# Norm 2's residual set by ScalarE in the projection's banks, tile 0's right half turned over DRAM, and the first gate/up products in another order

## The chip, the cores and the metric

One core of one Trainium2 chip runs one decoder layer for 256 tokens. The time is device microseconds of an execution, the median of several runs. TensorE is PE in the rows, VectorE DVE, ScalarE ACT, GpSimd POOL, and SP is SyncE, which issues the DMAs here. The page gives the clock that PE was granted in each slice of the span; in the kernel before it is the full one throughout.

## The reference, cut to what matters

`h` is (256, 1024) in float32, and so are all weights. The part that the change touches is the end of the cross-attention, the second norm and the beginning of the feed-forward layer:

```python
s = einsum('bshd,bmhd->bhsm', q, k) * (256 ** -0.5)      # 4 heads of 256, 256 memory tokens
p = softmax(s, axis=-1)
o = einsum('bhsm,bmhd->bshd', p, v).reshape(B, S, D)
h2 = layer_norm(DEEPNORM_ALPHA * h1 + o @ w_xo, ln2_g, ln2_b)
out = layer_norm(DEEPNORM_ALPHA * h2 + (silu(h2 @ w_gate) * (h2 @ w_up)) @ w_down, ln3_g, ln3_b)
```

`h1` is the output of the first norm, `D_FF` is 2816.

## The kernel before

**Tokens and products.** The 256 tokens are two tiles t of 128. A float32 product is made of three products of halves (L399 to L401): a matrix is split into a rounded high half (a ScalarE cast) and the rest, a low half (a VectorE subtraction), and high by high, low by high and high by low are summed in PSUM. `split` does this for activations (L527 on ScalarE, L528 on VectorE).

**Weights.** All weights come as one stream of numbered tiles w0, w1, ... of 128x1024 elements, 0.524 MB each. `Stream` loads a raw tile by a DMA on SyncE's queue (L125) into one of 7 raw buffers, splits it (`prepare`: ScalarE's cast L149, VectorE's subtraction L151) into one of 9 pairs of high and low tiles, and `refill` issues the load of the next raw tile into the buffer that the split frees. So w80's load waits for w73's low half, and w70's cast waits until TensorE has used w61 for the last time. `ws.late` keeps `refill` from running until it is called. Parameters of the norms (`ln2_g`, `ln2_b`, L369) are loaded on the same queue just ahead of given weights.

**The stages.** The four heads' queries are projected (`do_xq`), the scores of a head (`xscores`) go through a softmax, and its probabilities are transposed over DRAM: `xprobs_out` transposes blocks of 32 x 32 on VectorE (L560) and writes them, `xprobs_in` gathers them (xr) by four DMAs, `xprobs_split` makes the two halves xst, and `xattend` multiplies them with the values into the bank xo, which is split into oT. The output projection `project(c_xo, ...)` takes w51 to w58 into four banks acc, one for each piece: token tile 0 or 1, left or right half of the 1024 columns. With w51 to w54 it works on all four pieces at once, with w55 to w58 it finishes one piece after another. Then Norm 2 (`Norm`): for each piece the sum `alpha * h1 + acc` goes to r (L901), `bn_stats` measures it (L908, with a small addition at L910), `stats` joins both halves (L915) and GpSimd makes the reciprocal root (L917), `centre` (L922) and `scale` (L928) write h2.

**Gate and up.** h2 is needed transposed, as h2Th and h2Tl: eight TensorE transposes for tile 0 (L548), four for the left half of tile 1 (L538), while the right half of tile 1 is turned over DRAM (h2s, h2d, h2r). Gate and up are computed in chunks c of 256 columns each, chunk 0 with w59 to w62, chunk 1 with w63 to w66, chunk 2 with w67 to w70. `gated` makes silu(gate) times up (sg, L1188 and L1189), `gated_out` and `gated_in` turn it over DRAM (gs on VectorE, the write gd, four gathers gr at L571), `token_sums` makes sums of its blocks on GpSimd (L1208 to L1213), their split S goes into `shared_products`, with products of sums of the rows of w_down (w71, w72 for chunk 0) into four shared banks x.

**The order.** Each engine works through its instructions in the order in which this code issues them; there is no reordering. The generators (`project`, `proj_n`, `by_row`) issue some products at each step, so `run(gen, n)` followed by something else sets what stands behind what. `until(xo)` runs the projection until the next piece is finished. In the first chunks `run(gu, ...)` in the loop over c runs `by_row`, which goes through what is left of chunk 1, and `gated_in(0)` stands behind its third step.

## Time and profile before

| what | value |
|---|---|
| runs | 361.06, 361.18, 361.82 us; median 361.18 |
| profiled execution | 361.86 us, its span 360.1 |
| PE busy | 354.3 us (98%), 1768 instructions |
| DVE busy | 320.2 us (89%), 494 instructions |
| ACT busy | 208.6 us (58%), 335 instructions |
| POOL busy | 69.0 us (19%), 77 instructions |
| DMA | 90.80 MB, mean 252 GB/s |

The span is what the trace covers; 1.76 us of the execution lie around it. Times within the trace count from the start of the span. A matmul's start is measured and its end is modelled, so gaps on PE are read from one start to the next. An entry such as "[0.61 <-DVE xst L528]" behind an instruction says that its engine sat idle for 0.61 us before it, and that DVE's writing of xst at line 528 ended the wait.

### The profile page before, as it was taken

What the parts mean: (1) busy time and instruction counts of PE and PEld (TensorE: products, weight loads), DVE (VectorE), ACT (ScalarE), POOL (GpSimd) and SP (SyncE); (2) the same over time, 40 slices, a digit from 0 to 9 for tenths busy, and PEclk for the clock granted to TensorE, in tenths of its full rate; (3) what the DMA queues carried; (4) which work ended last, traced back from release to release, by engine and by line L of the source; (5) the groups of instructions that cost most, each with busy time, mean ns of one, the idle gap of its engine ahead of it and who ended that gap; (6) DMA issues with size and microseconds to landing.
All of it is one profiled execution on the core that took longest, in us unless ns stands there. A gap on an engine that the chain in (4) does not pass through costs nothing. (4 is left out here: it accounts for less than half of the span.)

```text
span 360.1 us, 5338 instructions
## 1 busy us (share of the span) xinstructions
PE 354.3 (98%) x1768; PEld 299.3 (83%) x1768; DVE 320.2 (89%) x494; ACT 208.6 (58%) x335; POOL 69.0 (19%) x77
## 2 busy tenths in 40 slices
PE   9999999999999999999999999999999999999995
PEld 8887888888888888988888888888888888888883
DVE  4888999987999877778999969999999999879995
ACT  5867775576363646557227627646744754675922
POOL 1000009400000000000010025044224304403284
PEclk9999999999999999999999999999999999999999
DMA  7997378799935955429918787697889889677113
GB/s 232 417 419 307 116 283 334 218 341 314 374 144 191 396 211 204 165 77 303 365 39 313 251 302 251 222 321 271 299 288 305 292 272 338 211 225 243 52 66 117
DMA packets 38748, 90.80 MB, mean 252 GB/s; under 512 B 4416, under 2 KB 16832, under 8 KB 38592
## 3 DMA queue, kind: packets, MB, share of 16 engines
q1 hardware_dynamic: 38288, 90.20, 70.7%
q8 instruction: 14, 0.23, 0.2%
q10 hardware_dynamic: 432, 0.26, 0.2%
q14 instruction: 14, 0.11, 0.1%
HBM read 82.58 MB, written 7.86 MB: 251 GB/s over the span
## 5 line engine op out<-in xcount | busy, mean ns | idle before, releaser
L1208 POOL TENSOR_TENSOR sraw<-gr 128x128 f32<-128x128 f32 x10 | 9.8, 976 | 103.2 <-DMA gr<-gd 63.6
L917 POOL TENSOR_TENSOR rs<-mv,mhalf 128x1 f32<-128x1 f32 x6 | 3.8, 634 | 115.0 <-DVE mv L915 115.0
L764 POOL TENSOR_TENSOR win<-upad 128x271 f32<-128x271 f32 x4 | 3.5, 882 | 52.3 <-DVE upad L801 52.3
L1188 ACT ACTIVATE sg<-pg 128x256 f32<-128x256 f32 x22 | 7.6, 379 | 5.9 <-PE pg L401 5.9
L1210 POOL TENSOR_TENSOR sraw<-gr 128x128 f32<-128x128 f32 x10 | 10.9, 1094 | 0.0
L528 DVE TENSOR_TENSOR gTl<-gr,gTh 128x512 fp32r<-128x512 f32 x11 | 8.9, 805 | 1.9 <-ACT gTh L527 1.9
L527 ACT CAST S<-sraw 128x384 fp32r<-128x384 f32 (+1 forms) x10 | 5.3, 533 | 8.5 <-POOL sraw L1210 8.5
L527 ACT CAST gTh<-gr 128x512 fp32r<-128x512 f32 x11 | 6.8, 615 | 4.5 <-DMA gr<-gd 4.5
L1209 POOL TENSOR_TENSOR sraw<-sraw,gr 128x128 f32<-128x128 f32 x10 | 9.2, 918 | 0.8
L1189 DVE TENSOR_TENSOR sg<-sg,pg 128x256 f32<-128x256 f32 x22 | 8.3, 412 | 0.1
L668 ACT ACTIVATE pr<-pr,mx 128x256 f32<-128x256 f32 (+1 forms) x12 | 5.5, 460 | 4.5 <-DVE mx L714 4.5
L560 DVE STREAM_TRANSPOSE gs<-sg 128x512 f32<-128x512 f32 x11 | 7.7, 702 | 0.1
L1213 POOL TENSOR_TENSOR S<-gr,sraw 128x128 f32<-128x128 f32 x8 | 7.5, 940 | 0.0
L922 DVE SCALAR_TENSOR_TENSOR r<-r,mv,g 128x512 f32<-128x512 f32 (+1 forms) x10 | 7.0, 729 | 0.2
L527 ACT CAST h2Th<-tp 128x512 fp32r<-128x512 f32 x3 | 1.7, 588 | 9.4 <-PE tp L548 6.7
L528 DVE TENSOR_TENSOR S<-sraw,S 128x384 fp32r<-128x384 f32 (+1 forms) x10 | 6.1, 606 | 1.0 <-ACT S L527 0.9
L165 POOL TENSOR_TENSOR w138l<-t,w138h 128x1024 fp32r<-128x1024 f32 x1 | 4.2, 4211 | 13.1 <-ACT w138h L164 13.1
L908 DVE BATCH_NORM_STATS2 st<-r 128x6 f32<-128x512 f32 (+1 forms) x10 | 6.4, 636 | 0.3
L1057 PE MATMUL xs<-xkTh,xq 128*128 128x256 f32 x32 | 6.4, 283 | 0.0
L527 ACT CAST h1T<-hr 128x512 fp32r<-128x512 f32 x4 | 2.3, 619 | 6.8 <-DMA hr<-hd 6.8
L527 ACT CAST xst<-xr 128x512 fp32r<-128x512 f32 x4 | 2.5, 619 | 6.3 <-DMA xd<-xs 3.6
L528 DVE TENSOR_TENSOR xst<-xr,xst 128x512 fp32r<-128x512 f32 x4 | 2.8, 688 | 3.8 <-ACT xst L527 3.8
(1390 smaller groups left out, 1378.9 us busy)
## 6 DMA issues: line engine op xcount, KB each, us to landing
gd<-gs SPq DMA_DIRECT2D x11, 256.0 KB, 5.8
gr<-gd SPq DMA_DIRECT2D x44, 64.0 KB, 2.0
pd<-ps SPq DMA_DIRECT2D x4, 384.0 KB, 4.1
pt<-pd SPq DMA_DIRECT2D x16, 96.0 KB, 5.7
g<-in_ln_g SPq DMA_DIRECT2D x3, 512.0 KB, 8.1
b<-in_ln_b SPq DMA_DIRECT2D x3, 512.0 KB, 9.6
wr<-in_w_qkv SPq DMA_DIRECT2D x5, 256.0 KB, 5.0
mr<-in_mem_t SPq DMA_DIRECT2D x1, 1024.0 KB, 11.8
```

The source lines that it names most:

```text
L527: nc.scalar.copy(h, ps)
L528: nc.vector.tensor_sub(l, ps, r32(h))
L560: nc.vector.transpose(st[:, :, at:at + m, :].rearrange("p j m b -> p m j b"), src.rearrange("p m (j b) -> p m j b", b=32))
L908: nc.vector.bn_stats(self.st[:, self.n, :], x)
L922: nc.vector.scalar_tensor_tensor(r, r, self.mv[:, 0:1], gb["g", self.i][:, s], op0=OP.subtract, op1=OP.mult)
L1057: nc.tensor.matmul(ps[:, t, :], w, xkT[n][:, 2 * h + kk], start=not (low or t or kk or n), stop=bool(low and kk), skip_group_check=True)
L1188: nc.scalar.activation(sg, ps[:, :CW].rearrange("p (f b) -> p f b", f=2), AF.Silu, bias=0.0, scale=1.0)
L1189: nc.vector.tensor_mul(sg, sg, ps[:, CW:].rearrange("p (f b) -> p f b", f=2))
L1208: nc.gpsimd.tensor_add(s1, a21, a22)
L1209: nc.gpsimd.tensor_sub(s2, s1, a11)
L1210: nc.gpsimd.tensor_sub(s3, a11, a21)
L1213: nc.gpsimd.tensor_sub(s4_raw, a12, s2)
```

## The change

Four things are changed together.

*The residual.* `residuals()` lets ScalarE write alpha times h1 into the four banks of the output projection before its first product, between the splits of the probabilities of heads 0 and 1; the projection then accumulates on top. The four sums L901 of Norm 2 are gone, and `bn_stats` and `centre` read the banks themselves. So that the banks are free, head 3's queries go to other ones, and the bank of head 2's scores is allocated ahead.

*Head 3.* `xprobs_split(3)` is issued ahead of the split of w60 instead of behind it.

*Tile 0's turn.* The right half of tile 0's h2 goes over DRAM as tile 1's does (`h2_out`, `landed`, `h2_split`), and four transposes instead of eight remain. The parameters of Norm 2 are loaded two and three weights earlier, and the load of w69 and w70 is issued behind the turn of tile 0.

*Order of gate and up.* Tile 0 of chunks 0 and 1 is interleaved in another way, the transposes of tile 1 move a few rows, and what is left of chunk 1's tile 0 (w65 and w66) is issued ahead of w61 and w62 of chunk 0's tile 1. `by_row` then has only tile 1 of chunk 1 left.

```diff
-    ws.before(c_gu[1][3], load_norm("g", 2, ln2_g))
-    ws.before(c_gu[2][0], load_norm("b", 2, ln2_b))
+    ws.before(c_gu[1][1], load_norm("g", 2, ln2_g))
+    ws.before(c_gu[1][2], load_norm("b", 2, ln2_b))
...
-        def centre(self, c0, c1, r=None):
+        def centre(self, c0, c1, r=None, src=None):
             s = slice(c0, c1)
             r = self.r[:, s] if r is None else r
-            nc.vector.scalar_tensor_tensor(r, r, self.mv[:, 0:1], gb["g", self.i][:, s],
+            nc.vector.scalar_tensor_tensor(r, r if src is None else src, self.mv[:, 0:1], gb["g", self.i][:, s],
...
-    def project(chunks, get, held, pieces=PIECES):
-        acc = {piece: accbank("acc") for piece in PIECES}
+    def project(chunks, get, held, pieces=PIECES, acc=None):
+        fresh = acc is None
+        if fresh:
+            acc = {piece: accbank("acc") for piece in PIECES}
...
-            yield from proj_rows(acc, head, get, PIECES, True, pieces != PIECES, True)
-        ws.prepare(ws.used + AHEAD)
+            yield from proj_rows(acc, head, get, PIECES, fresh, pieces != PIECES, True, not fresh)
+        if fresh:
+            ws.prepare(ws.used + AHEAD)
...
+    def residuals():
+        for piece in PIECES:
+            t, c0, c1 = piece
+            xo_acc[piece] = accbank("acc")
+            nc.scalar.mul(xo_acc[piece], h1[:, t, c0:c1], ALPHA)
...
+    ahead[2] = bank("xs")
     run(xq[3], 4)
     xprobs_split(0)
+    residuals()
     run(xq[3], 2)
     rest = xscores(2)
     xprobs_split(1)
...
     run(xo, 1)
+    xprobs_split(3)
     prepare()
     run(xo, 2)
-    xprobs_split(3)
-    prepare()
     xattend(2)
     xattend(3)
     prepare()
+    ws.late = True
+    prepare()
...
+    def h2_out(t):
+        return turned([(0, h2[:, t, 512:].rearrange("p (k b) -> p k b", k=4))], 4, "h2")
+    def h2_split(t, raw):
+        h, l = [half[:, 4:, t * P:(t + 1) * P].rearrange("p k (i b) -> p k i b", i=4) for half in h2T]
+        split(h, l, raw.rearrange("p i k b -> p k i b"))
...
-    for half in HALVES:
-        norm.add(*half, until(xo)[1])
-    norm.finish()
+    acc00 = until(xo)[1]
+    norm.take(acc00)
+    prepare()
+    acc01 = until(xo)[1]
+    norm.take(acc01)
+    norm.stats()
+    norm.centre(*RIGHT, src=acc01)
+    norm.centre(*LEFT, src=acc00)
+    norm.scale(*RIGHT)
+    turn0 = h2_out(0)
+    norm.scale(*LEFT)
...
+    turn0 = landed(turn0, 4, "h2")
+    ws.fetch(len(ws.raws) + 2, nc.sync)
     run(xo, 3)
-    norm.add(*HALVES[0], acc0)
-    transposes_tok(h2T, h2[:, 0, :], 0)
-    acc1 = until(xo)[1]
-    norm.add(*HALVES[1], acc1)
+    prepare()
+    transpose_tok(h2T, h2[:, 0, :], 0, 0, lambda: None)
+    acc11 = until(xo)[1]
+    run(xo)
+    norm.take(acc10)
+    norm.take(acc11)
     norm.stats()
...
+    norm.centre(*RIGHT, src=acc11)
+    norm.centre(*LEFT, src=acc10)
+    h2_split(0, turn0)
+    norm.scale(*RIGHT)
+    turn1 = h2_out(1)
+    norm.scale(*LEFT)
+    turn1 = landed(turn1, 4, "h2")
+    prepare()
+    ws.refill()
...
-    run(proj_n({0: first[0]}, c_gu[0], h2T, False, 2))
+    gu0 = proj_n({0: first[0]}, c_gu[0], h2T, False, 2)
+    run(gu0, 4)
     run(gu1[0], 4)
-    transpose_tok(h2T, h2[:, 1, :], 1, 0, lambda: (ws.prepare(ws.next()), gated(0, 0, first[0])))
-    run(gu1[0], 2)
-    gu0 = proj_n({1: first[1]}, c_gu[0], h2T)
+    run(gu0, 3)
+    transpose_tok(h2T, h2[:, 1, :], 1, 0, lambda: None)
+    run(gu0)
+    gated(0, 0, first[0])
+    gu0 = proj_n({1: first[1]}, c_gu[0], h2T, True, 2)
     run(gu0, 4)
-    ws.prepare(ws.next())
-    h, l = [half[:, 4:, P:].rearrange("p k (i b) -> p k i b", i=4) for half in h2T]
-    split(h, l, turn2.rearrange("p i k b -> p k i b"))
+    prepare()
+    run(gu1[0])
+    h2_split(1, turn1)
     ws.held = False
     run(gu0)
```

VectorE from the split of w60 to Norm 2 of tile 0; rows with + stand in the kernel after alone, with - in the one before alone; xst are head 3's probabilities, oT the heads' outputs:

```order
+L528 TENSOR_TENSOR xst<-xr,xst 128x512
 L151 TENSOR_TENSOR w60l<-w60r,w60h 128x1024
-L528 TENSOR_TENSOR xst<-xr,xst 128x512
+L528 TENSOR_TENSOR oTl<-xo,oTh 128x512 x2
 L151 TENSOR_TENSOR w61l<-w61r,w61h 128x1024
-L528 TENSOR_TENSOR oTl<-xo,oTh 128x512 x2
 L151 TENSOR_TENSOR w62l<-w62r,w62h 128x1024
+L908 BN_STATS st<-acc 128x6
+L910 TENSOR_SCALAR st<-st 128x1
 L151 TENSOR_TENSOR w63l<-w63r,w63h 128x1024
```

Head 3's low half moves ahead of w60's, both outputs' low halves ahead of w61's, and the first statistics ahead of w63's.

TensorE in chunk 0's tile 1, where w66 of chunk 1's tile 0 now ends and w61 follows:

```order
+L399 MATMUL pg<-w66h,h2Th 128x512
+L400 MATMUL pg<-w66l,h2Th 128x512
+L401 MATMUL pg<-w66h,h2Tl 128x512
 L399 MATMUL pg<-w61h,h2Th 128x512
 L400 MATMUL pg<-w61l,h2Th 128x512
 L401 MATMUL pg<-w61h,h2Tl 128x512
```

The six products of w66 for tile 0 stood behind w62's of tile 1 before, and now stand ahead of w61's and w62's.

SyncE's queue around the gathers of chunk 0 (gr from gd):

```order
 L125 DMA w78r<-in_w_down 128x1024
 L125 DMA w79r<-in_w_gu 128x1024
+L125 DMA w80r<-in_w_gu 128x1024
 L571 DMA gr<-gd 32x4x128 x4
-L125 DMA w80r<-in_w_gu 128x1024
 L125 DMA w81r<-in_w_gu 128x1024
```

w80's load was issued behind the four gathers and is now issued ahead of them.

## Rows read from the trace of the kernel before

**Rows 1.** Part 1 of the page: busy us (share of the span), instructions of each engine.

```profile
PE 354.3 (98%) x1768; PEld 299.3 (83%) x1768; DVE 320.2 (89%) x494; ACT 208.6 (58%) x335; POOL 69.0 (19%) x77
```

**Rows 2.** Timeline of PE at head 3: start, duration, engine, line, operation, out<-in, shape [idle].

```profile
165.73 0.28 PE L399 MATMUL xo<-xst,xv 128*128 128x256 f32 x1
166.62 0.39 PE L400 MATMUL xo<-xst,xv 128*128 128x256 f32 x1 [0.61 <-DVE xst L528]
166.85 0.28 PE L401 MATMUL xo<-xst,xv 128*128 128x256 f32 x1
...
167.92 0.28 PE L401 MATMUL xo<-xst,xv 128*128 128x256 f32 x1
```

**Rows 3.** Timeline of PE at the transposes of Norm 2's output (tp).

```profile
178.27 1.03 PE L548 MATMUL tp<-ident,h 128*128 128x128 f32 x8
179.06 0.48 PE L399 MATMUL acc<-w58h,oTh 128*128 128x512 f32 x1
...
179.84 0.39 PE L488 MATMUL pg<-w59h,h2Th 128*128 128x512 f32 x1
...
188.00 0.60 PE L538 MATMUL tp<-ident,h 128*128 128x128 f32 x4
188.36 0.48 PE L399 MATMUL pg<-w65h,h2Th 128*128 128x512 f32 x1
```

**Rows 4.** Timeline of ACT: casts of probabilities, outputs, a weight and transposed halves.

```profile
148.09 0.62 ACT L527 CAST xst<-xr 128x512 fp32r<-128x512 f32 x1 [2.69 <-DMA xr<-xd]
...
168.24 0.59 ACT L527 CAST oTh<-xo 128x512 fp32r<-128x512 f32 x1 [1.73 <-PE xo L401]
168.72 1.06 ACT L149 CAST w62h<-w62r 128x1024 fp32r<-128x1024 f32 x1
...
188.64 0.59 ACT L527 CAST h2Th<-tp 128x512 fp32r<-128x512 f32 x1 [2.78 <-PE tp L538]
...
190.69 0.62 ACT L527 CAST h2Th<-h2r 128x512 fp32r<-128x512 f32 x1 [0.51 <-DMA h2r<-h2d]
```

**Rows 5.** Timeline of DVE in Norm 2 of tile 0, and tile 1's transpose.

```profile
170.96 1.22 DVE L151 TENSOR_TENSOR w63l<-w63r,w63h 128x1024 fp32r<-128x1024 f32 x1
172.09 0.68 DVE L901 SCALAR_TENSOR_TENSOR r<-h,acc 128x512 f32<-128x512 f32 x1
172.80 0.70 DVE L908 BATCH_NORM_STATS2 st<-r 128x6 f32<-128x512 f32 x1
...
175.15 0.21 DVE L915 BATCH_NORM_AGGREGATE mv<-st 128x2 f32<-128x12 f32 x1
175.40 1.44 DVE L922 SCALAR_TENSOR_TENSOR r<-r,mv,g 128x512 f32<-128x512 f32 x2
176.76 1.40 DVE L928 SCALAR_TENSOR_TENSOR h<-r,rs,b 128x512 f32<-128x512 f32 x2
...
184.58 0.71 DVE L560 STREAM_TRANSPOSE h2s<-h 128x512 f32<-128x512 f32 x1
```

**Rows 6.** Timelines of all five engines on the way to chunk 0's sums S.

```profile
194.13 1.06 ACT L149 CAST w70h<-w70r 128x1024 fp32r<-128x1024 f32 x1
195.71 1.21 DVE L151 TENSOR_TENSOR w70l<-w70r,w70h 128x1024 fp32r<-128x1024 f32 x1
...
203.13 1.21 DVE L151 TENSOR_TENSOR w73l<-w73r,w73h 128x1024 fp32r<-128x1024 f32 x1
...
204.81 1.80 SPq L571 DMA_DIRECT2D gr<-gd  x4
...
210.34 0.46 POOL L1208 TENSOR_TENSOR sraw<-gr 128x128 f32<-128x128 f32 x1 [26.71 <-DMA gr<-gd]
...
212.78 0.56 DVE L528 TENSOR_TENSOR S<-sraw,S 128x384 fp32r<-128x384 f32 x1 [0.90 <-ACT S L527]
...
214.10 0.39 PE L401 MATMUL x<-w71h,S 128*128 128x512 f32 x1
```

**Rows 7.** Windows: us, busy (count) of PE, PEld, DVE, ACT, POOL, PEclk, DMA share, GB/s.

```profile
203.00:212.00 9.00, 9.00 (x41) 7.48 (x40) 6.98 (x9) 3.73 (x6) 1.58 (x3) 1.00 0.85 275
```

More of the change, by code (lines that the diff above doesn't have):

```diff
@@ L956, in project @@
             yield from proj_rows(acc, rest, lambda k: get(done + k), [piece], not head or piece[1] % 512 != 0, True,
-                                 piece == pieces[-1], bool(head) and pieces != PIECES)
+                                 piece == pieces[-1], bool(head) and (pieces != PIECES or not fresh))
             yield piece, acc[last] if pieces != PIECES and piece == pieces[-2] else acc[piece]
@@ L1038, in do_xq @@
     def do_xq(h):
-        pss = [halved((accbank if h else bank)("pxq")) for f in range(2)]
+        pss = [halved((accbank if h in (1, 2) else bank)("pxq")) for f in range(2)]
         yield from proj_w(pss, c_xq[h], h1T)
@@ L1048, in do_xq @@
         split(*xqT[h], sums)
+    ahead, xo_acc = {}, {}
+    def residuals():
[3 more added lines that the diff above has]
+            nc.scalar.mul(xo_acc[piece], h1[:, t, c0:c1], ALPHA)
     def xscores(h):
-        ps = bank("xs").rearrange("p (t s) -> p t s", t=2)
+        ps = (ahead.pop(h, None) or bank("xs")).rearrange("p (t s) -> p t s", t=2)
         for low in range(2):
@@ L1130, in decoder_layer @@
     h2 = ap.tile([P, T, D], F32, tag="a8", name="h2")
-    xo = project(c_xo, lambda k: (oT[0][:, k], oT[1][:, k]), 4)
+    xo = project(c_xo, lambda k: (oT[0][:, k], oT[1][:, k]), 4, acc=xo_acc)
     xattend(0)
@@ L1156, in decoder_layer @@
     prepare()
+    ws.late = True
+    prepare()
     h2T = (a8("h2Th", F32R), a8("h2Tl", F32R))
     gT = [(a8(f"gTh{i}", F32R), a8(f"gTl{i}", F32R)) for i in range(3)]
[L1161 to L1164 removed]
+    LEFT, RIGHT = HALVES
+    def h2_out(t):
[3 more added lines that the diff above has]
+        split(h, l, raw.rearrange("p i k b -> p k i b"))
+    norm = Norm(2, h1[:, 0, :], h2[:, 0, :])
+    acc00 = until(xo)[1]
[9 more added lines that the diff above has]
+    norm.scale(*LEFT)
     norm = Norm(2, h1[:, 1, :], h2[:, 1, :])
[L1166 removed]
+    acc10 = until(xo)[1]
     warm = sp.tile([P, 32], F32, name="warm", bufs=1)[:, :1]
     nc.scalar.activation(warm, mhalf, AF.Silu, bias=0.0, scale=1.0)
+    turn0 = landed(turn0, 4, "h2")
+    ws.fetch(len(ws.raws) + 2, nc.sync)
     run(xo, 3)
[L1170 to L1182 removed]
+    prepare()
[4 more added lines that the diff above has]
+    norm.take(acc11)
+    norm.stats()
+    norm.centre(*RIGHT, src=acc11)
[7 more added lines that the diff above has]
+    ws.refill()
     def gated(c, t, ps):
@@ L1262, in decoder_layer @@
     sgs = [sp.tile([P, 2, T, P], F32, name="sg", tag="pr", bufs=PR_BUFS)]
-    first = [accbank("pg") for t in range(T)]
-    second = [accbank("pg") for t in range(T)]
+    first, second = zip(*[[accbank("pg") for n in range(2)] for t in range(T)])
     gu1 = [proj_n({t: second[t]}, c_gu[1], h2T, t == 1) for t in range(T)]
-    run(proj_n({0: first[0]}, c_gu[0], h2T, False, 2))
+    gu0 = proj_n({0: first[0]}, c_gu[0], h2T, False, 2)
+    run(gu0, 4)
     run(gu1[0], 4)
-    transpose_tok(h2T, h2[:, 1, :], 1, 0, lambda: (ws.prepare(ws.next()), gated(0, 0, first[0])))
-    run(gu1[0], 2)
-    gu0 = proj_n({1: first[1]}, c_gu[0], h2T)
+    run(gu0, 3)
[3 more added lines that the diff above has]
+    gu0 = proj_n({1: first[1]}, c_gu[0], h2T, True, 2)
     run(gu0, 4)
-    ws.prepare(ws.next())
-    h, l = [half[:, 4:, P:].rearrange("p k (i b) -> p k i b", i=4) for half in h2T]
-    split(h, l, turn2.rearrange("p i k b -> p k i b"))
+    prepare()
+    run(gu1[0])
+    h2_split(1, turn1)
     ws.held = False
```

8 lines of the change are left out of this document (removed).

## The prediction

> **What bounds the kernel now.** I read the page first: TensorE is busy for 354.3 us of a span of 360.1 [rows 1], so it sets the time, and anything else counts only where it makes TensorE wait or takes instructions from it. Then I went through TensorE's timeline for gaps between the starts of its products. In the stretch that the change touches they follow each other every 0.227 us (512 columns; some 40 in 9.00 us, where [rows 7] counts 41 with those cut at the ends) or 0.12 us (256 columns: half of that, and 0.01) with one exception: at head 3 of the cross-attention a product starts 0.89 us after the one before it, named as waiting for VectorE's low half of the probabilities, and the next comes 0.23 us later instead of 0.12 [rows 2]. The transposes of the Norm 2 output are the other thing there that is not a product [rows 3]. From there I followed each input of the stretch back through the timelines of ScalarE, VectorE, SyncE's queue and GpSimd, to see how much later it could come without TensorE noticing. The profiled execution took 361.86 us, its span 360.1, so 1.76 lie around it; it is 0.68 above the median of 361.18. I take differences within the execution and add them to the median. 0.2%, about what a measurement of this kernel can tell from no change, is 0.72 us.
>
> **What it takes off TensorE.** (1) Head 3's probabilities are split one weight tile earlier on ScalarE and VectorE. The low half before started only behind the low half of w60; now it ends about where that one started its last part, before TensorE comes to it. The exception goes: 0.89 − 0.12 and 0.23 − 0.12 make 0.77 + 0.11 = 0.88 us [rows 2]. (2) Four of eight transposes of tile 0 go to the DMA: eight took from 178.27 to 179.06, 0.79 us, four from 188.00 to 188.36, 0.36 us [rows 3]; so 0.43 us. Together −1.31.
>
> **What costs nothing.** The four scaled copies of h1 into the projection's banks are about 0.6 us each by the nearest row, a ScalarE cast of 512 (0.59 to 0.62 us), 2.4 in all; they stand behind the cast of head 0, ahead of which ScalarE idled 2.69 us waiting for its data [rows 4], and what follows them on ScalarE is a cast whose data also lands only later. If that cover were gone they would hold the products of head 0's neighbours by up to 2.4 us, but all of it would have to be exposed at once. The four sums on VectorE go (0.68 us each, [rows 5]); VectorE has no way to pass that on directly, it only starts its next step earlier. The gate/up products are the same in number, so their new order is worth something only through waits.
>
> **What it adds: transposes behind Norm 2.** (3) The last product of head 3 started at 167.92 [rows 2]; without the stall it starts at 167.04, and the transposes would come at 178.27 − 0.88 = 177.39. Norm 2 of tile 0 on the other engines then runs so: ScalarE's cast of head 3's output follows the product by 0.32 us as before (168.24 − 167.92), 167.36; w61's high half, which now stands behind it instead of ahead, 0.48 later (168.72 − 168.24), 167.84 [rows 4]; its low half when that cast of 1.06 is done, 168.93; two low halves of 1.13 each (170.96 to 172.09), 171.2; statistics 0.73 (0.70 and the 0.03 between instructions); the small addition 0.18 (what is left of 172.80 to 175.15 after two statistics of 0.73 and one sum of 0.71); w63's low half 1.13; statistics 0.73; aggregate 0.25 (175.15 to 175.40); two centres 1.36 (175.40 to 176.76); one scale 0.70; the new 32 x 32 transpose 0.63 to 0.71 (184.58's row); one scale 0.70 [rows 5]. The left half is there at 177.7 to 177.8. Wait 0.4, and after a wait the first product cost 0.11 extra [rows 2]: 0.5 us. Bounds: 0, if ScalarE or VectorE gets one step ahead of this, and 0.8, if a weight's cast slips by a third of its 1.06. A gain is excluded, as nothing is taken away here that (1) and (2) have not counted.
>
> [...]
>
> (4) Behind each of the two groups of four transposes TensorE has one row of three products of other data and then needs the ScalarE cast of what was transposed. The cast started 0.64 us behind the transposes (188.64 − 188.00) and takes 0.59 [rows 3, 4]; with 0.06 to the product, 1.29 us. TensorE gets there after 0.36 + 0.78 = 1.14 us (179.06 to 179.84 are the three products, [rows 3]). Wait 0.15, with the 0.11 of a restart 0.25, twice 0.5 us; bounds 0 and 0.8. So far TensorE: −0.88 − 0.43 + 0.5 + 0.5 = −0.3.
>
> The right half of tile 0 goes over SyncE's queue: five DMAs, ahead of two weight loads. By the row of the gathers of chunk 0 four issues take 1.80 us [rows 6], and for tile 1's right half, which went this way before, 6.1 us lay between the start of its transpose at 184.58 and the cast of what landed, which began at 190.69 [rows 4, 5]. From the new transpose at 176.3 that makes 182.4; it is needed behind 24 products of gate/up, which begin some 1.4 behind the transposes, at 177.8 + 1.4 + 24 × 0.227 = 184.6: no wait. Weights w69 and w70 move back behind the turn, to some 181, and w70 is cast only at 194.13 [rows 6].
>
> **What it adds: chunk 0's token sums come later.** (5) This is where I see the result decided. Today the low half of the sums S of chunk 0 is done at 212.78 + 0.56 = 213.34, and TensorE uses it at 214.10: 0.76 us to spare [rows 6]. That alone caps any gain ahead of it: with 0.06 to the product and 0.11 of a restart TensorE can't be there more than about 0.6 earlier unless S comes earlier too. And S comes later, for two reasons. First, six products of w66 (1.36 us) now stand ahead of w61's last use, which comes 1.36 − 0.3 = 1.06 later. w70's cast waits for that buffer; it started at 194.13, as that product ended, and will at 195.19; its low half follows after its 1.06, at 196.25 instead of 195.71: VectorE's row through w73's low half, done at 204.34, moves by +0.5 [rows 6]. Second, the order on SyncE's queue: w80's load, which waits for w73's low half to free its raw buffer, now stands ahead of chunk 0's four gathers, which were issued at 204.81 and landed when GpSimd began at 210.34. They can now be issued only at 204.34 + 0.5 + 0.45 (one issue, a quarter of 1.80) = 205.3, +0.5, and w80's 0.524 MB are ahead of them. Price of that: nothing, if the DMA engines carry both side by side (they were 85% busy here), up to 0.524 MB / 275 GB/s = 1.9 us, if the gathers wait for all of it at this stretch's rate [rows 7]. The gathers took 5.5 us from issue to landing though they are small, so they do stand behind other loads, yet they are spread over four issues; I take the middle, +1.0. Landing +1.5 (bounds 0.5 and 2.4), S low at 214.84. TensorE's own path brings it there at 214.10 − 0.3 = 213.8: wait 214.84 + 0.06 − 213.8 = 1.1, with the restart 1.2. Sum: −0.3 + 1.2 = **+0.9 us**, with the bounds −0.1 (landing +0.5: wait 0.2) and +1.8 (landing +2.4: wait 2.1). Since S decides, the terms (1) to (4) hardly enter the result: whatever TensorE saves ahead it waits for here. Later chunks have more to spare, and TensorE is back to back behind, so I carry +0.9 to the end.
>
> [...]
>
> **Rivals.** A: w80's load doesn't hold the gathers up and VectorE's row makes up part of the 0.5. Then S costs 0 to 0.2 and the change is worth its TensorE terms, −0.1 to −0.6, about 360.9. For it: the DMA engines have 15% to spare and SyncE only waits some 0.5 longer. Against: 5.5 us for small gathers. B, on the other side: the waits (3) and (4) don't arise and S doesn't bind, −1.3, 359.9. The point from which it decides: S must be ready by 214.10 − 1.31 = 212.79, 0.55 earlier than today, so the gathers must land by 209.7, although they are issued later; only an emptier queue at 203 us could do that. For it: the raw loads are kept back around Norm 2, so fewer may be in flight; against: 275 GB/s there [rows 7] and the same bytes before it. [...] D: the change doesn't do what it says, head 3's split still being late because its data, by its own turn over DRAM, lands too late for the earlier place. Then up to 0.88 stay and w61, w73 and S move with them: +0.9 + 0.88 = +1.8, 363.0. For it: the split moves up by a whole weight tile. Against: before, ScalarE's cast of it had no wait of its own that the trace names.
>
> **How the numbers follow.** Forecast (S decides, w80's load in the way) 0.53, A 0.25, B 0.13, C 0.05, D 0.04. The predicted time is 361.18 + 0.9 = 362.1; that case alone spans 361.1 to 363.0. The range, 360.5 to 363.0, takes in A and leaves out most of B and the far end of D. Slower by over 0.72 us: two thirds of the forecast (0.35), C and most of D, 0.43. Faster by over 0.72: B and a little of A, 0.15. The rest, 0.42, within.
>
> **What would show it.** Right: no gap at head 3's products; four transposes; waits of some tenths ahead of the first transposes and ahead of the first product on each transposed half; the gathers issued behind w80, landing near 211.8; a wait of about 1 us at the first product with S's low half. Wrong: S's low half there in time (A, B), the gathers landing where they landed before, or a wait in a place that I have not named, above all later, where VectorE has the least to spare.

## The result

The changed kernel is slower: a median of 363.32 us (8 executions, 362.62 to 365.23) beside 361.62 for the kernel before (8 executions, 361.06 to 362.99), a ratio of 1.0054 with a 95% interval of 1.003 to 1.0077, or 1.1 to 2.8 us. The forecast was 362.1 with a range of 360.5 to 363.0: slower was the likelier side, but the size was about half of it, and the range ends too low.

In the profiled execution of the changed kernel the span is 361.7 us, 1.6 more than before. TensorE's timeline (start, duration, engine, line, operation, out<-in, shape, and in brackets the idle time and what ended it) shows the waits that were added, one after the other; the transposes, its second row, answer to 178.27 in [rows 3]:

```profile
177.33 0.39 PE L401 MATMUL acc<-w57h,oTl 128*128 128x512 f32 x1
177.89 0.63 PE L538 MATMUL tp<-ident,h 128*128 128x128 f32 x4 [0.17 <-DVE h L928]
178.28 0.48 PE L399 MATMUL acc<-w58h,oTh 128*128 128x512 f32 x1
...
178.82 0.40 PE L401 MATMUL acc<-w58h,oTl 128*128 128x512 f32 x1
179.20 0.50 PE L488 MATMUL pg<-w59h,h2Th 128*128 128x512 f32 x1
179.53 0.40 PE L488 MATMUL pg<-w59l,h2Th 128*128 128x512 f32 x1
...
212.53 0.39 PE L401 MATMUL pg<-w70h,h2Tl 128*128 128x512 f32 x1
213.50 0.50 PE L399 MATMUL x<-w71h,gTh 128*128 128x512 f32 x1 [0.58 <-ACT gTh L527]
213.83 0.40 PE L400 MATMUL x<-w71l,gTh 128*128 128x512 f32 x1
214.52 0.50 PE L401 MATMUL x<-w71h,gTl 128*128 128x512 f32 x1 [0.29 <-DVE gTl L528]
215.38 0.50 PE L399 MATMUL x<-w71h,S 128*128 128x512 f32 x1 [0.35 <-ACT S L527]
...
217.69 0.39 PE L399 MATMUL pg<-w73h,h2Th 128*128 128x512 f32 x1
```

In the kernel before, the same stretch runs from the last product of w70 to the first of w73 without a wait:

```profile
212.74 0.39 PE L401 MATMUL pg<-w70h,h2Tl 128*128 128x512 f32 x1
212.97 0.39 PE L399 MATMUL x<-w71h,gTh 128*128 128x512 f32 x1
...
215.69 0.39 PE L399 MATMUL pg<-w73h,h2Th 128*128 128x512 f32 x1
```

In the changed kernel the transposes start 0.56 after the product ahead of them, where 0.23 would do; the first product of w59 starts 0.38 behind its neighbour. These are tenths. At 212.53 the large loss begins: from there to the first product of w73 TensorE took 5.16 us for what took 2.95 in the kernel before. Three of the changed kernel's rows name the releaser, and all three come from one source: chunk 0's gathers, whose data makes gTh, gTl and S. How late they were stands in SyncE's queue (start, duration of the issue, line, transfer); of before, 204.81 in [rows 6] answers to the last of these:

```profile
204.02 1.06 SPq L125 DMA_DIRECT2D w79r<-in_w_gu  x1
205.17 0.38 SPq L125 DMA_DIRECT2D w80r<-in_w_gu  x1
205.66 1.89 SPq L571 DMA_DIRECT2D gr<-gd  x4
```

And on GpSimd's timeline, where 210.34 in [rows 6] answers to it:

```profile
212.93 0.46 POOL L1245 TENSOR_TENSOR sraw<-gr 128x128 f32<-128x128 f32 x1 [30.73 <-DMA gr<-gd]
```

GpSimd begins 2.59 later than before, and 7.3 us behind the first issue instead of 5.5. The DMA view gives the time from issue to landing (last number, us) of the load that stands last ahead of the gathers, first w79's in the kernel before, then w80's in the changed one:

```profile
w79r<-in_w_gu SPq DMA_DIRECT2D x1, 512.0 KB, 5.9
```

```profile
w80r<-in_w_gu SPq DMA_DIRECT2D x1, 512.0 KB, 6.7
```

Issued at 203.24 and at 205.17, they landed at 209.16 and 211.84, and each time the first gather landed 0.29 behind that load. It is so in all traces with loads under way ahead of the gathers: the first of the four lands 0.17 to 0.41 us after the last load ahead of it.

And on VectorE, w73's low half, which frees w80's raw buffer, starts at 203.91 instead of 203.13, because something held this engine earlier (timeline of VectorE):

```profile
183.95 0.69 DVE L528 TENSOR_TENSOR h2Tl<-h2r,h2Th 128x512 fp32r<-128x512 f32 x1 [1.00 <-ACT h2Th L527]
184.56 0.75 DVE L928 SCALAR_TENSOR_TENSOR h<-r,rs,b 128x512 f32<-128x512 f32 x1
185.34 0.71 DVE L560 STREAM_TRANSPOSE h2s<-h 128x512 f32<-128x512 f32 x1
...
203.91 1.22 DVE L151 TENSOR_TENSOR w73l<-w73r,w73h 128x1024 fp32r<-128x1024 f32 x1
```

It waits 1.00 us for tile 0's half that was turned over DRAM, with tile 1's scale and transpose standing behind it, so that tile 1's half goes out at 185.34 instead of 184.58 [rows 5], and what follows shifts by that.

Since executions begin at slightly different times and end with stores of different length, the runs below are compared by TensorE's path: from the first product with w11 (27.1 to 27.8 us in the traces) to the start of its last product. The columns are worked out from the starts in each trace: the path; what of it is a wait at L751 and L752, in the self-attention, whose code is the same in all; the stretch from the last product of w70 to the first of w73; and from the last product to the end of the span. All but the first column of numbers are in us.

| kernel | time to before (95% interval) | path | at L751 | w70 to w73 | behind it |
|---|---|---|---|---|---|
| before | 1 | 328.64 | 0 | 2.95 | 4.33 |
| before_2, before_3 | | 328.04, 328.80 | 0, 0 | 2.95, 2.95 | 4.33, 4.34 |
| changed | 1.0054 (1.003 to 1.0077) | 330.27 | 0 | 5.16 | 4.21 |
| after_2 | | 333.17 | 1.00 | 6.60 | 4.17 |
| gather_first | 1.002 (1.001 to 1.0031) | 329.63 | 1.62 | 2.95 | 4.40 |
| gather_later | 1.0163 (1.0147 to 1.0178) | 333.81 | 0 | 7.65 | 4.17 |
| scale_first | 1.0054 (1.0038 to 1.0071) | 330.85 | 0 | 5.77 | 4.18 |
| both | 1.0014 (1.0004 to 1.0023) | 328.64 | 0 | 3.25 | 4.40 |
| early_gather | 1.0001 (0.9992 to 1.001) | 328.42 | 0.32 | 2.95 | 4.39 |
| before_late | 1.006 (1.0041 to 1.0079) | 329.19 | 0.24 | 4.13 | 5.22 |
| head3_only, head3_again | 1.0016 (1.0007 to 1.0025), 1.0021 (1.0006 to 1.0036) | 327.75, 328.67 | 0, 0 | 2.95, 2.95 | 5.23, 5.19 |
| head3_pad | 1.0001 (0.999 to 1.0013) | 328.81 | 0 | 2.95 | 4.31 |
| before_pad | 0.999 (0.998 to 1.0) | 327.76 | 0 | 2.95 | 4.31 |
| residual_only | 1.0021 (1.0012 to 1.003) | 328.52 | 0 | 2.95 | 4.40 |
| early_w63 | 1.004 (1.0027 to 1.0053) | 329.07 | 0 | 2.95 | 4.40 |
| early_w63_split | 1.0022 (1.0004 to 1.004) | 328.72 | 0 | 2.95 | 4.40 |

### The profile page after: what moved, and what is told of

It is laid out like the page before. It is cut to its first block, busy times and chain, and to the rows that moved or that the text cites. A ratio compares the mean times of both kernels' runs of the same rounds, so it can differ in the third digit from the quotient of the medians.

```text
span 361.7 us, 5342 instructions
## 1 busy us (share of the span) xinstructions
PE 355.3 (98%) x1764; PEld 298.6 (83%) x1764; DVE 318.0 (88%) x491; ACT 210.6 (58%) x339; POOL 65.0 (18%) x77
## 5 line engine op out<-in xcount | busy, mean ns | idle before, releaser
L1245 POOL TENSOR_TENSOR sraw<-gr 128x128 f32<-128x128 f32 x10 | 9.8, 984 | 108.5 <-DMA gr<-gd 78.6
L1247 POOL TENSOR_TENSOR sraw<-gr 128x128 f32<-128x128 f32 x10 | 10.0, 995 | 0.0
L1246 POOL TENSOR_TENSOR sraw<-sraw,gr 128x128 f32<-128x128 f32 x10 | 7.5, 754 | 0.8
L764 POOL TENSOR_TENSOR win<-win 128x269 f32<-128x269 f32 (+2 forms) x6 | 5.8, 972 | 0.5
L928 DVE SCALAR_TENSOR_TENSOR h<-r,rs,b 128x512 f32<-128x512 f32 x8 | 5.7, 733 | 0.0
L908 DVE BATCH_NORM_STATS2 st<-acc 128x6 f32<-128x256 f32 (+1 forms) x10 | 5.2, 530 | 0.3 <-PE acc L1458 0.3
L1046 ACT ACTIVATE xqs<-pxq 128x256 f32<-128x256 f32 x8 | 2.6, 383 | 4.8 <-PE pxq L466 4.8
L1493 ACT ACTIVATE r<-r,rs 128x512 f32<-128x512 f32 x2 | 1.3, 716 | 7.0 <-POOL rs L917 7.0
```

The source lines that it names most:

```text
L764: nc.gpsimd.tensor_add(nxt[:, 2 * n - 1:], cur[:, 2 * n - 1:], cur[:, n - 1:PADW + S - n])
L928: nc.vector.scalar_tensor_tensor(self.dst[:, s], r, self.rs, gb["b", self.i][:, s], op0=OP.mult, op1=OP.add)
L1245: nc.gpsimd.tensor_add(s1, a21, a22)
L1246: nc.gpsimd.tensor_sub(s2, s1, a11)
L1247: nc.gpsimd.tensor_sub(s3, a11, a21)
```

## Experiments on the gathers' place in the queue

Theory Q: the gathers are late because w80's load stands ahead of them in SyncE's queue. Its rivals: VectorE is late (V), or more bytes are in flight whatever the order (D).

**gather_first.** The gathers are issued one step of `by_row` earlier, which puts them ahead of w80 again:

```diff
-        run(gu, 2)
+        run(gu, 1)
         if c == 1:
             gated_in(0)
+        run(gu, 1)
```

> The changed kernel with chunk 0's four gathers issued ahead of w80's load again, as in the kernel before; nothing else differs. Theory Q (the queue's order): of the 2.6 us by which the gathers land later than in the kernel before, the part behind w80 (about 1.7) goes; they are issued at about 205.2 and land at about 210.7, S's low half is there at 213.8, TensorE's 2.3 us of extra waiting at chunk 0's shared products shrink to 0.3 or less, and the time is that of the kernel before, within 0.4 us. Theory V (VectorE was late, the queue's order does nothing): the landing stays at about 212.5 and the time at about 1.5 above the kernel before. Theory D (more bytes in flight, whatever the order): the same as V.

Measured: 1.002. The gathers went out at 206.58, and GpSimd began 5.0 us later instead of 7.3. SyncE's queue:

```profile
206.58 1.80 SPq L571 DMA_DIRECT2D gr<-gd  x4
208.48 0.38 SPq L125 DMA_DIRECT2D w80r<-in_w_gu  x1
```

GpSimd's timeline:

```profile
211.57 0.46 POOL L1245 TENSOR_TENSOR sraw<-gr 128x128 f32<-128x128 f32 x1 [27.86 <-DMA gr<-gd]
```

(This execution had lost 1.62 us at L751 already, so its times are that much later than the others'.) TensorE passes from w70 to w71 without a wait, the stretch is 2.95 again: Q, against V and D. The time, expected within 0.4 of the kernel before, stays 0.7 above it; what is left is taken up below.

**before_late.** The other way round: the kernel before with nothing but its gathers one load later.

```diff
         run(gu, 2)
         if c == 1:
+            run(gu, 1)
             gated_in(0)
```

> The kernel before with nothing but chunk 0's gathers issued one load later, behind w80's. Theory Q (one load ahead of the gathers is the cause): they are issued about 0.5 later, land 2.2 to 2.5 us later, and with the 0.76 us that S had to spare TensorE waits some 1.5 to 1.8 in all at the shared products: the time is 1.4 to 1.8 above the kernel before, nearly the whole of what the change cost. If it is the release of w61's buffer or the later turn of tile 1 that counts in the changed kernel: 0.3 at most.

Measured: 1.006, as slow as the changed kernel. w80 is issued at 204.19, the gathers at 204.88, and GpSimd begins 7.0 us later, at 211.91. On TensorE's timeline:

```profile
212.78 0.39 PE L399 MATMUL x<-w71h,gTh 128*128 128x512 f32 x1
213.00 0.39 PE L400 MATMUL x<-w71l,gTh 128*128 128x512 f32 x1
213.51 0.49 PE L401 MATMUL x<-w71h,gTl 128*128 128x512 f32 x1
214.36 0.50 PE L399 MATMUL x<-w71h,S 128*128 128x512 f32 x1 [0.36 <-ACT S L527]
```

The stretch grows by 1.18 us, so the order alone makes a wait of that size. It isn't the whole of the time, though: 0.9 of it lies behind TensorE's last product (5.22 instead of 4.33), which the section on the tail explains.

**gather_later.** The changed kernel with the same edit as before_late, so that w80 and w81 stand ahead.

> The changed kernel with chunk 0's gathers one load further back, behind w81's too. Theory Q: another load ahead of them costs about as much as the first, 1.3 to 1.9 us; landing at about 214.4, the time about 3.3 above the kernel before. Theories V and D: landing later by the issue alone, 0.4 to 0.5, and the time 2.1 above the kernel before.

Measured: 1.0163, 5.8 us, more than any theory said, while GpSimd began only 0.7 later on TensorE's path than in the changed kernel (at 213.44, in an execution that began 0.19 earlier). So a second load ahead did not cost as much as the first, against theory Q's own price: issued at 206.41, the gathers again took 7.0 us. w81's load, the last ahead of them, landed at 212.20, only 0.4 after w80's in the changed kernel, and the first gather 0.26 behind it: the price here was what was still on its way at the issue, not so much for each load. The rest is the clock. The windows view of this run (us, busy time and count of PE, PEld, DVE, ACT and POOL, the granted clock, DMA share, GB/s):

```profile
208.00:213.00 5.00, 4.72 (x21) 3.57 (x19) 1.48 (x2) 0.00 (x0) 0.00 (x0) 1.00 1.04 314
213.00:217.00 4.00, 2.25 (x6) 1.32 (x7) 1.74 (x3) 1.65 (x3) 2.27 (x4) 0.79 0.65 246
217.00:219.00 2.00, 2.00 (x6) 1.61 (x5) 1.90 (x4) 0.28 (x1) 0.58 (x1) 0.50 0.22 64
219.00:222.00 3.00, 3.00 (x8) 2.32 (x8) 2.96 (x4) 3.00 (x6) 2.99 (x3) 0.50 0.00 0
222.00:225.00 3.00, 3.00 (x14) 2.42 (x14) 3.00 (x5) 2.68 (x4) 0.06 (x1) 0.97 0.77 238
```

TensorE had done 2.25 us of work in the four from 213 to 217, where the changed kernel's profile shows 2.86 and the full clock; from 217 until about 222 it was granted 0.50 of its clock, and the windows from 217 to 222 hold 6 and 8 products where those of the kernel before hold 10 and 15.

**early_gather.** The changed kernel with w76 and w77 held back until chunk 0's write and its gathers are issued (and with the edit of scale_first, below):

```diff
-        self.fetch(max(self.freed, len(self.homes)) + RAW_BUFS, self.nc.sync)
+        self.fetch(min(max(self.freed, len(self.homes)) + RAW_BUFS, self.limit or len(self.src)), self.nc.sync)
...
     prepare()
+    ws.limit = 76
     ws.refill()
...
     gated_out(0)
+    gated_in(0)
+    ws.limit = None
+    ws.refill()
...
-        if c == 1:
-            gated_in(0)
```

> The changed kernel with tile 1's scale ahead of tile 0's split, and the loads of w76 and w77 held back until chunk 0's write and its four gathers have been issued, so that neither stands behind more than w75. If the queue is what held chunk 0: the write lands about 2 us after its issue instead of 5.8, the gathers at about 204 to 205, 5 us earlier than in the kernel before; S is ready before TensorE, and TensorE's own terms are kept: 0.4 to 0.6 below the kernel before. If S is bound by something else on VectorE or GpSimd, the time is that of the run with both edits, 0 to 0.5 above the kernel before; if w76 to w78, loaded some 6 us later, are missed, it is slower than that.

Measured: 1.0001. With an empty queue ahead of them the write (issued at 199.04) has landed and the gathers go out 2.05 us later, and GpSimd begins 3.6 behind that. SyncE's queue:

```profile
199.04 0.33 SPq L563 DMA_DIRECT2D gd<-gs  x1
201.09 1.75 SPq L571 DMA_DIRECT2D gr<-gd  x4
202.94 0.38 SPq L125 DMA_DIRECT2D w76r<-in_w_gu  x1
```

GpSimd's timeline:

```profile
204.64 1.04 POOL L1246 TENSOR_TENSOR sraw<-gr 128x128 f32<-128x128 f32 x1 [22.08 <-ACT w74h L149]
```

That is 5.7 us earlier than in the kernel before, although the write was issued no earlier (at 198.03 there, landing 5.3 us later). Q is settled. The time, however, only comes back to that of the kernel before; the 0.4 to 0.6 below it didn't appear.

## Experiments on VectorE

**scale_first.** The split of tile 0's turned half stands behind tile 1's scale and transpose:

```diff
-    h2_split(0, turn0)
     norm.scale(*RIGHT)
     turn1 = h2_out(1)
+    h2_split(0, turn0)
     norm.scale(*LEFT)
```

> The changed kernel with the split of tile 0's turned half issued behind tile 1's right scale and its 32 x 32 transpose, instead of ahead of them; the gathers stay behind w80. Theory V: VectorE no longer waits 1.00 us for tile 0's turned data ahead of tile 1's scale, tile 1's half lands 0.76 earlier, and so do w67 to w73, the gathers and S: the time falls by 0.7 against the changed kernel, about 1.0 above the kernel before. If only the queue's order counts: VectorE's row moves, but the landing doesn't, and the time stays at 1.7 above.

Measured: 1.0054, no change against the changed kernel. VectorE no longer waits there, but another wait has taken its place ahead of w73. VectorE's timeline:

```profile
196.72 1.23 DVE L151 TENSOR_TENSOR w70l<-w70r,w70h 128x1024 fp32r<-128x1024 f32 x1 [0.62 <-ACT w70h L149]
...
204.16 1.22 DVE L151 TENSOR_TENSOR w73l<-w73r,w73h 128x1024 fp32r<-128x1024 f32 x1
```

ScalarE's timeline:

```profile
195.63 1.06 ACT L149 CAST w70h<-w70r 128x1024 fp32r<-128x1024 f32 x1 [1.16 <-PE pg L401]
```

This execution began 0.38 later than that of the changed kernel, so w73's low half stands only 0.13 earlier. w70's cast waits 1.16 us for TensorE's last use of w61, which is the release that the prediction named; in the changed kernel it is hidden behind the later landing. By these rows two causes stand in parallel, and taking away one gains nothing; a run without both isn't there. The gathers took 8.1 us in this execution, the longest of all traces, so its stretch of 5.77 is no price of the edit.

**both.** The edits of gather_first and scale_first.

> Both of these edits: gathers ahead of w80, and tile 1's scale and transpose ahead of tile 0's split. If V and Q add up: landing at about 210.0, as early as in the kernel before or earlier, no wait at S, and what is left are TensorE's own terms, 0.2 to 0.6 below the kernel before. If a third cause holds S (the release of w61's buffer, the bytes in flight), the landing stays at 210.7 or later, and the time at the kernel before's or above.

Measured: 1.0014. The gathers are issued at 205.14, in an execution that began 0.25 later than that of the kernel before, so nearly as early, and GpSimd begins at 211.1; TensorE comes to w71 0.41 us earlier on its path than in the profile before and gives 0.31 of it back there (3.25 instead of 2.95). That is the cap that the prediction spoke of. The path as a whole is that of the first profile before.

## Experiments on the parts

**head3_only.** The kernel before with nothing but `xprobs_split(3)` ahead of w60's split:

```diff
     run(xo, 1)
+    xprobs_split(3)
     prepare()
     run(xo, 2)
-    xprobs_split(3)
     prepare()
```

> The kernel before with nothing but head 3's split issued ahead of w60's split, so that the low half of its probabilities is there before TensorE comes to it. Theory Q (S of chunk 0 caps any gain ahead of it): the 0.88 us at head 3 go, and all that stands behind runs that much earlier until chunk 0's shared products, where at most about 0.6 is kept, as the gathers still land near 210.3; the time falls by 0.3 to 0.6. If the gathers move along with the rest, by 0.88. If the order of w60's split costs elsewhere, no change.

Measured: 1.0016, slower, though TensorE's path is 0.89 shorter than in the profile before, as expected. So the gathers did not stay where they were (S was split 0.34 earlier on the path, and with its spare time the stretch stayed at 2.95), nor did the time follow the path. That the 0.89 are the edit's work isn't shown: before_pad, which leaves head 3 as it was, has the same path, 327.76.

**residual_only.** The kernel before with nothing but the residual. `project` with banks that are given to it also leaves out one `ws.prepare`, as in the changed kernel.

```diff
+    residuals()
...
-    xo = project(c_xo, lambda k: (oT[0][:, k], oT[1][:, k]), 4)
+    xo = project(c_xo, lambda k: (oT[0][:, k], oT[1][:, k]), 4, acc=xo_acc)
...
-    norm.add(*HALVES[0], acc0)
+    norm.take(acc0)
```

> The kernel before with nothing but the residual: ScalarE writes alpha times h1 into the four banks ahead of the projection, the four sums of VectorE go, statistics and centring read the banks. As the prediction has it: nothing on TensorE's path, time within 0.2 of the kernel before; the Norm 2 steps on VectorE run 0.7 to 1.4 us earlier, and the statistics and centres of 512 take the 0.70 us that they took from SBUF. [...]

Measured: 1.0021, slower by 0.76. The residual itself costs nothing: no wait up to w63. But w63 and w64 are split later, as the left-out `prepare` would have taken them earlier, and TensorE waits for w63's low half, 0.40 from one product to the next instead of 0.23, and for w64's, 0.54 (TensorE's timeline):

```profile
184.57 0.39 PE L399 MATMUL pg<-w63h,h2Th 128*128 128x512 f32 x1
184.97 0.50 PE L400 MATMUL pg<-w63l,h2Th 128*128 128x512 f32 x1
...
186.23 0.40 PE L399 MATMUL pg<-w64h,h2Th 128*128 128x512 f32 x1
186.77 0.50 PE L400 MATMUL pg<-w64l,h2Th 128*128 128x512 f32 x1
```

In the changed kernel these splits have places of their own, and it doesn't have this wait. On VectorE's timeline, the statistics and centres that read the banks:

```profile
173.00 0.70 DVE L908 BATCH_NORM_STATS2 st<-acc 128x6 f32<-128x512 f32 x1 [1.83 <-PE acc L401]
173.74 0.21 DVE L915 BATCH_NORM_AGGREGATE mv<-st 128x2 f32<-128x12 f32 x1
173.98 1.41 DVE L922 SCALAR_TENSOR_TENSOR r<-acc,mv,g 128x512 f32<-128x512 f32 x2
```

0.70 and 1.41, beside 0.70 and 1.44 from SBUF [rows 5]. Neither operation took longer from the banks.

## The kernel before, and the changed one, once more

**before_2, before_3, after_2.** Both kernels as they are, for further profiles.

> The kernel before, unchanged, for a second profile. If the 0.88 us at head 3 belong to the kernel: there again, the product 0.89 behind the one before it. If they belong to the one execution (there, the write of head 2's probabilities took from 151.79 until 156.57, in the profiles of kernels with the same order here 2.3 to 3.5 us): no gap at head 3 where that write is quick, and TensorE's path from the first product of w11 to its last is 327.8 instead of 328.6 us.

> The kernel before, unchanged, for a third profile; the same question as for the second.

> The changed kernel, unchanged, for a second profile. If the gathers behind w80 are the cause in every execution: again a wait of 1.5 to 2.5 us at chunk 0's shared products, and the waits of 0.33 and twice 0.15 at the transposes. If it was one execution: the gathers land near 211 and the wait is under 1.

At head 3, where the first profile has 0.89 us from one product to the next [rows 2], the second has 0.17 (165.92 to 166.09) and the third 0.61. TensorE's timeline in before_2:

```profile
165.92 0.28 PE L399 MATMUL xo<-xst,xv 128*128 128x256 f32 x1
166.09 0.39 PE L400 MATMUL xo<-xst,xv 128*128 128x256 f32 x1
```

And in before_3:

```profile
166.76 0.28 PE L399 MATMUL xo<-xst,xv 128*128 128x256 f32 x1
167.37 0.39 PE L400 MATMUL xo<-xst,xv 128*128 128x256 f32 x1 [0.33 <-DVE xst L528]
```

In before_late, before_pad and residual_only, which have the same order there, it is gone. What differs is how soon SyncE's next gathers can go out behind the write of head 2's probabilities. This write was issued at 151.79 in the first profile of the kernel before and the gathers followed at 156.57, 4.78 us later; it is 4.04 in before_2, 4.46 in before_3, 3.45 in before_pad, 2.48 in residual_only and 2.33 in before_late. There is no stall up to 3.45 and it grows from 4.04 on, so the 0.88 us are what a slow write costs in that execution; over the six profiles with this order they are 0.88, 0.6, 0.15 and three times nothing, 0.27 in the mean.

after_2 took 366.91 us. The loss at the gathers is there again (GpSimd 7.4 us behind the first issue), now with 1.07, 0.46 and 0.63 us of waits at w71, and TensorE's clock fell after them (windows of after_2, columns as above; 0.80 and 0.56 are means over a change: from 218.54 to 221.10 the products start 0.42 to 0.43 apart, instead of 0.23):

```profile
213.00:217.00 4.00, 2.68 (x10) 1.36 (x8) 0.99 (x1) 0.95 (x2) 2.13 (x4) 1.00 1.03 367
217.00:219.00 2.00, 1.77 (x6) 1.24 (x7) 1.75 (x3) 0.70 (x2) 0.05 (x1) 0.80 0.29 106
219.00:222.00 3.00, 3.00 (x9) 2.36 (x8) 2.90 (x5) 2.01 (x5) 0.79 (x2) 0.56 0.23 66
```

In its first profile the clock was 1.00 in all these windows, with 0.74, 0.46 and 0.63 us of waits. The two executions of the changed kernel at 365.0 and 365.2 us had a mean clock of 0.994, the six others 0.998 or 0.999, so they too lost clock; only after_2, with 0.995, has a trace that shows where.

## Experiments on the tail

head3_only left a riddle, a shorter path and a longer time. Its span has 5.23 us behind TensorE's last product, the kernel before 4.33. In both traces one packet of 8 KB of the instruction queue falls into the end: at 356.55 in the kernel before, ahead of the last store's packets, which end 1.7 us after its last issue; at 357.60 in head3_only, among them, and they end 2.6 us after.

**head3_again, head3_pad, before_pad.** The same kernel for a second profile; the same with eight additions of 128x1 in VectorE's idle time at chunk 0's gathers; and the kernel before with these eight alone.

```diff
-    mhalf = cp.tile([P, 96], F32, name="mhalf")[:, :1]
+    spare = cp.tile([P, 96], F32, name="mhalf"); mhalf = spare[:, :1]
...
+            for n in range(8 if c == 2 else 0):
+                nc.vector.tensor_scalar(spare[:, 8 + n:9 + n], mhalf, D * EPS, None, op0=OP.add)
             gated_split(c - 2)
```

> The run with head 3's split alone, once more, for a second profile. In the first, TensorE's last product started 0.89 earlier than in the kernel before, but the last packets of the final store ended 2.6 us after its issue instead of 1.7, with an 8 KB code packet at 357.6 among them; the time was 0.6 above the kernel before. If that packet comes at a fixed place of the program: again within the final store, and the time again 0.3 to 0.8 above. If it was an accident of one execution: a tail as before's, and 0.5 to 0.9 below.

> The same with eight additions of 128 x 1 on VectorE in its idle time at chunk 0's gathers, which move every later instruction of VectorE by eight places in its code. If the place of the last code packet is set by VectorE's code: it comes several us earlier, in time that TensorE bounds, the final store takes its 1.7 us, and the time is 0.5 to 0.9 below the kernel before. If not: the same as without the eight.

> The kernel before with the same eight additions and nothing else, as a control. If they only shift code: within 0.2 of the kernel before, with the last code packet at another time. If the additions themselves cost: slower.

Measured: 1.0021, 1.0001 and 0.999. In head3_again the packet comes at 358.49, again within the store, and 5.19 us lie behind the last product; with the eight additions it comes at 350.8 and 350.2, and 4.31 lie there. So VectorE's code moves this packet, and its place goes with 0.9 us of the tail: of all traces just head3_only, head3_again and before_late have it within the store, and they alone have 5.2 there (4.2 to 4.4 in the others). The path of head3_again and head3_pad is not the 327.75 of head3_only: both have a new wait, at the low half of the heads' output, 0.49 and 0.54 us: TensorE, no longer held at head 3, comes to it before VectorE, which has w61's low half ahead of it. In both the write of head 2's probabilities took 4.31 us; in head3_only, without that wait, 2.49. So head 3's move alone gains nothing that can be measured once the tail is equal (1.0001, where 0.5 to 0.9 us were expected). The control, expected within 0.2 us, is 0.4 faster by its ratio, at the edge of its interval; its tail is that of the kernel before, and what makes it faster, if anything does, isn't shown.

## Two attempts at a better version

**early_w63, early_w63_split.** early_gather with w63's split moved out of Norm 2 of tile 0 to behind its left scale, and w64's behind the split of the transposed half; the second with tile 0's turned half split where the changed kernel has it.

```diff
     norm.take(acc00)
-    prepare()
...
     norm.scale(*LEFT)
+    prepare()
...
-    prepare()
     transpose_tok(h2T, h2[:, 0, :], 0, 0, lambda: None)
+    prepare()
```

> The same, with w63's split moved out of Norm 2 of tile 0 to behind its left scale, and w64's behind the split of the transposed left half. The transposes of tile 0 then don't wait (0.33 + 0.1 in the changed kernel): 0.8 to 1.0 below the kernel before. If w63 or w64 then come too late for chunk 1's first products, the wait is only moved, and the time is that of the run before this one.

> The changed kernel with the early gathers and with w63's split behind Norm 2's left scale of tile 0, but with tile 0's turned half split ahead of tile 1's right scale, as the changed kernel has it. The 1.27 us that TensorE waited at w61 for that half's low part in the run before it should go, since it is done one scale and one transpose (1.4) earlier: TensorE's path then has the two waits behind the transposes alone (0.25 each) against the 0.43 of four transposes, and the time is 0 to 0.4 below the kernel before. If the low part still comes late, up to 0.5 above.

Measured: 1.004 and 1.0022. The wait ahead of tile 0's transposes is gone in both, and each time a larger or equal one has come: 1.27 us at w61 for the low part of tile 0's turned half in the first; in the second the 0.42 us have moved to tile 1's transposes. No version here beats the kernel before beyond doubt; early_gather and head3_pad equal it, and before_pad, which changes nothing but the place of its code, is at 0.999 with an interval that ends at 1.0.

## Why the prediction was right or wrong, step by step

**Right: where it is decided.** The loss is at chunk 0's shared products, by the gathers behind w80, as the part "chunk 0's token sums come later" said; gather_first and early_gather take it away, and before_late makes it in the kernel before.

**Right: the terms on TensorE, to a tenth or so, against the profile they were read from.** Up to the last product of w70 the changed kernel's path is 0.37 shorter than the profile before; the sum had −0.3. The stall at head 3 is gone (−0.86 of the −0.88), four transposes are saved, the transposes wait 0.33 (0.4), and behind each group TensorE waits 0.15 and restarts with 0.11 (0.25 each), as rows 178.82 to 179.53 show. (The rows that the prediction adds up for the left half of Norm 2 come to 177.6 to 177.7, not to its 177.7 to 177.8; the scale ended at 177.75.)

**The step that failed: "I take the middle, +1.0".** The price of w80's load ahead of the gathers was 1.7 to 1.8 us: 5.5 from the first issue to GpSimd's beginning in the kernel before, 7.3 in the changed one. (Over all traces with loads under way it is 5.0 to 6.6 without one more load ahead and 7.0 to 8.1 with it.) With the later issue (+0.85, of which 0.15 is a later beginning of the execution; the prediction had +0.5) that makes a landing 2.4 later on the path, the upper bound; put into the sum as it stood it gives +1.8, and the path at w73 is 1.85 longer. By the landings shown above the gathers waited for the whole of the last load ahead, the first landing 0.29 behind it in both profiles. The middle between two bounds was chosen without a row that lies near the middle; the row nearest to the case, a gather that takes 5.5 us because it stands behind other loads, spoke for the upper end. gather_first against the changed kernel agrees with that end (5.0 against 7.3 us), and with that end the forecast would have been 363.0, an estimate with the prediction's own upper bound.

**A part that failed in its reason.** The shift of VectorE's row was put at +0.5, by w61's release. It was 0.63 on the path (0.78 in the rows, less the later beginning), by a wait that I had excluded: "no wait" was argued for tile 0's turned half from TensorE's need alone, though VectorE's split of it stands ahead of tile 1's scale in its order. It landed at 183.3 instead of 182.4 and TensorE was not held by it, but VectorE was, for 1.00 us. The release of w61 is real and stands just behind (scale_first).

**What the range left out.** Three things. The median that the forecast was added to, 361.18 from three executions, is 0.44 below that of the eight, 361.62. Then, two executions with longer waits lost clock for some microseconds behind them (after_2, granted 0.80 and 0.56 in the windows from 217 to 222, and gather_later, granted 0.50 there); the sum counted waits at their length. And the sum's first term, −0.88, was read in one execution; in five further profiles with that order this stall is 0.15 in the mean. Other short waits can stand in its place (before_3 has 0.49 at the scores, L1057, and a path of 328.80), but the term did not belong to the kernel, and that TensorE's terms came out as forecast against the first profile was the luck of that execution. In before_pad, which has no such wait, TensorE's path is 184.78 from the first product with w11 to the last of w70; the changed kernel's 185.27 is 0.49 longer, not 0.37 shorter, for the waits behind the transposes take more than four transposes save. That would also account for most of what gather_first and both stay above the kernel before, 0.6 to 0.7, with no wait left at the gathers in the one and 0.3 in the other; that it is the whole of it isn't shown.

**The rivals.** A and B needed gathers that landed in time: no. C, to which the forecast gives 0.05, is that VectorE takes longer where it reads the projection's banks: no run shows that, and in residual_only one statistics instruction took 0.70 us and two centres 1.41, beside 0.70 and 1.44 from SBUF [rows 5]. D, head 3's data too late for its new place: not in the changed kernel's two profiles, with writes of 4.3 and 4.0 us, but the wait that head3_again and head3_pad show is of that kind.

**Open.** Why the last code packet falls into the final store in head3_only and before_late, whose VectorE programs are as long as that of the kernel before, isn't known. Nor was each of the four parts run alone: tile 0's turn and the order of gate and up weren't.

## What to carry to other kernels

Here the first of four gathers of 64 KB landed 0.17 to 0.41 us behind the last load of 0.524 MB ahead of it, and one more load ahead cost 1.7 to 1.8 us (the changed kernel): before an order of issues changes, even by one load, look what its queue holds at that time and take the whole of what is still on its way as the price. Behind a wait on an engine look for what stands in its order, not only for who needs the result; here tile 0's early split, waiting 1.00 us, held tile 1's scale. And a stall that a single profile shows belongs to the kernel only when a second execution has it too.

## What the runs showed of the hardware

TensorE's clock: after waits of 1.07, 0.46 and 0.63 us (after_2) it was granted 0.80 and then 0.56 in the windows up to 222 us, after 0.74, 0.46 and 0.63 us (the changed kernel's first profile) it stayed at 1.00; gather_later lost about 2.7 us of path by it, worked out as its 3.5 above the changed kernel less the 0.8 that it came later from the last product of w70 to the first with S (3.64 instead of 2.85).

Code loading: in the three traces that have one 8 KB packet of the instruction queue inside the final store, the kernel ends 0.9 us later (5.2 instead of 4.3 us behind the last product), half of what the change cost; eight additions of 128x1 on VectorE moved the packet out, and the 0.9 us went with it.

The write of 0.26 MB to DRAM that a gather waits for took 2.05 us until the gathers went out where the queue was empty, and for the write of the same size with head 2's probabilities between 2.3 and 4.8 from one execution to the next.

Where four gathers of 64 KB were issued on SyncE's queue with loads of 0.524 MB under way, the first landed 0.17 to 0.41 us after the last of the loads ahead, whether that was w79's, w80's or w81's (209.16, 211.84 and 212.20 in before, after and gather_later); with none under way the first of the four took 1.8 us (early_gather).
